# Softmax cross-entropy, first load cut at partition 16, labels behind the table load, last sums in PSUM with refitted pieces

## The chip, the cores and the metric

One core of one Trainium2 chip. The metric is the device time of one execution in microseconds. Runs of the kernel before on one chip agree within about 0.6 us in 2431 (0.03%). By the record's 95% intervals (about 0.15% to either side of a ratio) effects of a few tenths count as no difference; they are read here from five rounds and from traces, and are only as sure as that.

In the profile's lines ACT is ScalarE, DVE is VectorE, POOL is GpSimd and SP the engine that issues the logit loads. HBM is the memory that the logits come from; SBUF and PSUM are the core's two on-chip memories. A packet is what one DMA engine moves in one piece, here a row's part of a load. A load lands when its last byte is reported in.

## The reference

```python
batch, seq, vocab = 16, 512, 32000          # fp32 logits, labels
logits_max = np.max(logits, axis=-1, keepdims=True)
log_sum_exp = np.log(np.sum(np.exp(logits - logits_max), axis=-1)) + logits_max.squeeze(-1)
log_probs = logits - log_sum_exp[..., np.newaxis]
loss = -log_probs[np.arange(batch)[:, None], np.arange(seq), labels]
```

1.05 GB of logits are read once; the result is 8192 numbers. The kernel leaves out the maximum (the logits are normal draws).

## The kernel before

The 8192 rows are split over 128 partitions, 64 rows each ("groups" g = 0..63). Row p*64+g goes to partition p, so a load takes 128 rows that lie 8.19 MB apart. Groups are loaded in two halves of 16000 columns into three buffers in turn; ScalarE does exp in place and sums each half with its accumulator. The loads of the first group and of the last two are shorter.

```python
P = 128; G = 64; W = 16000
lg_pg = lg.rearrange("(p g) v -> p g v", g=G)

plan(0, [[4000, 4000, 8000], [16000]], [(0, 0), (0, 1), (0, 2), (1, 0)])
for g in range(1, G - 2):
    plan(g, [[W], [W]], [(0, 0), (1, 0)])
for g, i, at, n in [                          # group, buffer, column in it, width
    (G - 2, 0, 0, 12000), (G - 2, 1, 0, 11000), (G - 2, 2, 0, 9000),
    (G - 1, 3, 0, 8720), (G - 1, 2, 9000, 6470), (G - 1, 3, 8720, 4700),
    (G - 1, 4, 0, 3410), (G - 1, 3, 13420, 2550), (G - 1, 4, 3410, 1910), (G - 1, 4, 5320, 1455),
    (G - 1, 4, 6775, 1135), (G - 1, 4, 7910, 905), (G - 1, 4, 8815, 745),
]: ...
sums = persist.tile([P, G - 1, 5], FP32)      # SBUF
sums_last = persist.tile([P, K], FP32)        # SBUF, K = 10
nc.scalar.dma_start(out=labs64[:], in_=labels_pg)
nc.scalar.preload_act_table_set("natural_log_exp_and_others")
nc.vector.memset(sums[:], 0.0)
# ... gathers, index lists (cut)
for j, (g, b, at, n) in enumerate(loads):
    load = nc.sync.dma_start(out=t[:, at:at + n], in_=lg_pg[:, g, c0:c0 + n])
    # ... semaphores, pick of the label's logit (cut)
    nc.scalar.activation(out=ap, in_=ap, func=EXP, accum_out=s)
    if left == 1:
        nc.vector.reduce_sum(out=part[:], in_=sums_last[:, 0:K - 1], axis=X)
nc.scalar.activation(out=logsum_last[:], in_=sums_last[:, K - 1:K], func=LN, bias=part[:])
# ... subtract, store (cut)
```

The softmax here doesn't subtract the row's maximum and nothing guards it: scores larger than these inputs give would overflow.

Of the kernel before, what the change touches and what calls it, by code (L numbers as in the profile page):

```python
# [9 lines left out]
FP32 = mybir.dt.float32  # L10
# [4 lines left out]
LN = mybir.ActivationFunctionType.Ln  # L15
ALU = mybir.AluOpType
X = mybir.AxisListType.X
# [3 lines left out]
def kernel(  # L21
# [6 lines left out]
    nc = tc.nc  # L28

    B, S, V = logits.shape  # L30
    P = 128
    G = B * S // P
    W = 16000
# [3 lines left out]
    lg_pg = lg.rearrange("(p g) v -> p g v", g=G)  # L37
# [7 lines left out]
    def plan(g, widths_by_buffer, order):  # L45

        n_buffers = 1 + max((l[1] for l in loads), default=-1)
        for b, i in order:
            ws = widths_by_buffer[b]
            loads.append((g, n_buffers + b, sum(ws[:i]), ws[i]))  # L50

    plan(0, [[4000, 4000, 8000], [16000]], [(0, 0), (0, 1), (0, 2), (1, 0)])
    for g in range(1, G - 2):
        plan(g, [[W], [W]], [(0, 0), (1, 0)])
    b = loads[-1][1] + 1
    for g, i, at, n in [
        (G - 2, 0, 0, 12000), (G - 2, 1, 0, 11000), (G - 2, 2, 0, 9000),
        (G - 1, 3, 0, 8720), (G - 1, 2, 9000, 6470), (G - 1, 3, 8720, 4700),
        (G - 1, 4, 0, 3410), (G - 1, 3, 13420, 2550), (G - 1, 4, 3410, 1910), (G - 1, 4, 5320, 1455),
        (G - 1, 4, 6775, 1135), (G - 1, 4, 7910, 905), (G - 1, 4, 8815, 745),  # L60
    ]:
        loads.append((g, b + i, at, n))
    assert sum(l[3] for l in loads) == G * V
# [2 lines left out]
    persist = ctx.enter_context(tc.tile_pool(name="persist", bufs=1))  # L66
# [24 lines left out]
    own = persist.tile([P, NB * 2, NI], FP32)  # L91
# [1 line left out]
    in_first = persist.tile([P, G], mybir.dt.int32)  # L93
    picks = ctx.enter_context(tc.tile_pool(name="picks", bufs=2))
    K = 10
    sums = persist.tile([P, G - 1, 5], FP32)
    sums_last = persist.tile([P, K], FP32)
    totals = persist.tile([P, G - 1], FP32)
    logsum = persist.tile([P, G - 1], FP32)
    res = persist.tile([P, G - 1], FP32)  # L100
    part = persist.tile([P, 1], FP32)
    logsum_last = persist.tile([P, 1], FP32)
    res_last = persist.tile([P, 1], FP32)

    ctx.enter_context(tc.manual_schedule())


    nc.scalar.dma_start(out=labs64[:], in_=labels_pg)
    nc.scalar.preload_act_table_set("natural_log_exp_and_others")  # L109
    nc.vector.memset(sums[:], 0.0)  # L110
    nc.gpsimd.iota(idx[:], pattern=[[V, G]], base=0, channel_multiplier=G * V)
    nc.gpsimd.tensor_tensor(out=idx[:], in0=idx[:], in1=labs32, op=ALU.add)  # L112
    nc.gpsimd.iota(part16[:], pattern=[[0, 1]], base=0, channel_multiplier=1)
    nc.gpsimd.iota(entries[:], pattern=[[1, NI]], base=0, channel_multiplier=0, allow_small_or_imprecise_dtypes=True)
    for g in gathered:
        nc.gpsimd.indirect_dma_start(  # L116
            out=lab_logit[:, g:g + 1],
            out_offset=None,
            in_=lg,
# [6 lines left out]
    for q in range(3):  # L126
        nc.vector.tensor_scalar(  # L127
            out=mine[:, q:q + 1], in0=part16f[:], scalar1=4.0 * q, scalar2=None, op0=ALU.add
        )
    for n in (12.0, 6.0):  # L130
        nc.vector.tensor_scalar(  # L131
            out=mine_at[:], in0=mine[:], scalar1=n, scalar2=n, op0=ALU.is_ge, op1=ALU.mult
# [3 lines left out]
    for q in range(3):  # L136
        nc.vector.tensor_scalar(  # L137
            out=mine_at[:, q:q + 1], in0=mine[:, q:q + 1], scalar1=16.0 * q, scalar2=None, op0=ALU.mult
# [4 lines left out]
        out=one_hot[:], in0=entries[:], scalar1=at_entry[:], scalar2=None, op0=ALU.is_equal  # L143
    )
    nc.vector.tensor_scalar(
        out=clamped[:, 0, :], in0=labs32, scalar1=float(W - 1), scalar2=None, op0=ALU.min
    )
    nc.vector.tensor_scalar(
        out=clamped[:, 1, :], in0=labs32, scalar1=float(-W), scalar2=0.0, op0=ALU.add, op1=ALU.max
    )  # L150
    nc.vector.tensor_scalar(
        out=in_first[:], in0=labs32, scalar1=float(W), scalar2=None, op0=ALU.is_lt
    )
    for h in range(2):
        for q in range(3):
            nc.vector.tensor_scalar(  # L156
                out=lists[:, :, h, q], in0=clamped[:, h, :], scalar1=mine[:, q:q + 1], scalar2=None, op0=ALU.mult
# [6 lines left out]
    buffers = {}  # L164
    col = {}
    n_exp = {}
    full_in = [tc.alloc_semaphore(f"full{i}_in") for i in range(3)]
    n_full = [0, 0, 0]
    spaces = [data.tile([P, W], FP32, tag=f"t{i}", name=f"t{i}") for i in range(3)]
    exps = []  # L170

    def exp(g, ap):
        k = n_exp.get(g, 0)
        n_exp[g] = k + 1
        s = sums[:, g, k:k + 1] if g < G - 1 else sums_last[:, k:k + 1]
        return nc.scalar.activation(out=ap, in_=ap, func=EXP, accum_out=s)  # L176

    for j, (g, b, at, n) in enumerate(loads):
        if b not in buffers:
            buffers[b] = spaces[b % 3]  # L180
        t = buffers[b]
        c0 = col.get(g, 0)
        col[g] = c0 + n
        load = nc.sync.dma_start(out=t[:, at:at + n], in_=lg_pg[:, g, c0:c0 + n])  # L184
        if n == W:
            n_full[b % 3] += 1
            loaded = (full_in[b % 3], 16 * n_full[b % 3])
        else:
            loaded = (tc.alloc_semaphore(f"short{j}_in"), 16)
        load.then_inc(loaded[0], 16)  # L190
        tc.no_tile_sem_insts.add(load.ins.name)
        users = []
        if g in picked:
            h = c0 // W
            i = picked.index(g) % NB
            if h == 0 and i == 0:
                pk = picks.tile([P, NB * 2, NI], FP32, tag="pk", name="pk")
            pick = nc.gpsimd.indirect_copy(  # L198
                out=pk[:, 2 * i + h, :], data=t[:], idxs=lists[:, g, h, 0:3], i_know_this_is_slow=True
            )  # L200
            users.append(pick)
        users.append(exp(g, t[:, at:at + n]))
        users[0]._wait_ge(*loaded)
        tc.add_to_no_dep_group(f"load{j}", load.ins)
        tc.declare_no_dep(users[0].ins, load.ins, reason="waits for the load's own semaphore")
        tc.declare_fence(users[0].ins, group=f"load{j}")
        exps.append(users[-1])
        if g in picked and h == 1 and i == NB - 1:
            nc.vector.copy_predicated(own[:], one_hot[:].unsqueeze(1).to_broadcast([P, NB * 2, NI]), pk[:])  # L209
            nc.vector.reduce_sum(  # L210
                out=found[:, :, g - NB + 1:g + 1].rearrange("p h g -> p g h"),
                in_=own[:].rearrange("p (g h) n -> p g h n", h=2),
                axis=X,
            )

        left = len(loads) - 1 - j
        if left == 9:
            nc.vector.reduce_sum(out=totals[:], in_=sums[:], axis=X)  # L218
            lo, hi = picked[0], picked[-1] + 1
            nc.vector.tensor_copy(out=lab_logit[:, lo:hi], in_=found[:, 1, lo:hi])  # L220
            nc.vector.copy_predicated(lab_logit[:, lo:hi], in_first[:, lo:hi], found[:, 0, lo:hi])  # L221
        if left == 8:
            nc.scalar.activation(out=logsum[:], in_=totals[:], func=LN)  # L223
            nc.vector.tensor_tensor(out=res[:], in0=logsum[:], in1=lab_logit[:, 0:G - 1], op=ALU.subtract)  # L224
        if left == 1:
            nc.vector.reduce_sum(out=part[:], in_=sums_last[:, 0:K - 1], axis=X)  # L226
    assert n_exp[G - 1] == K
    nc.sync.dma_start(out=out_pg[:, 0:G - 1], in_=res[:])

    nc.scalar.activation(out=logsum_last[:], in_=sums_last[:, K - 1:K], func=LN, bias=part[:])  # L230
    nc.vector.tensor_tensor(out=res_last[:], in0=logsum_last[:], in1=lab_logit[:, G - 1:G], op=ALU.subtract)  # L231
    nc.sync.dma_start(out=out_pg[:, G - 1:G], in_=res_last[:])

# [29 lines left out]
```

## Time and profile before

| | before |
|---|---|
| time, median (runs) | 2430.91 us (6) |
| span of the profiled run | 2428.7 us |
| share of the span that the logit queue holds the DMA engines | 99.9% |
| last landing of logits | 2424.71 us |

The GB/s row of the page cuts the span in 40 slices of 60.7 us; a slice shows what the engines moved. It is flat from the first slice on, so the start and the end are the only places where anything can be won or lost.

```profile
GB/s 423 438 422 438 438 424 437 438 433 427 438 437 423 439 436 426 436 438 432 428 438 435 425 438 436 428 434 436 434 428 436 437 426 436 437 429 433 436 430 383
```

The same start in wider windows (DMA share and GB/s stand last; a packet is booked where it starts):

```profile
5.00:10.00 5.00, 0.99 (x8) 1.90 (x1) 1.27 (x4) 1.00 1.03 440
10.00:20.00 10.00, 3.52 (x19) 5.36 (x4) 3.40 (x4) 1.00 1.04 440
30.00:40.00 10.00, 0.00 (x0) 0.00 (x0) 0.00 (x0) 1.00 0.95 410
```

### The profile page before, as it was taken

The numbers are of one execution on the slowest core, as the hardware profiler recorded it, in microseconds if no ns is written. First come the engines' busy times: TensorE is split into PE (matmuls) and PEld (weight loads), VectorE is DVE, ScalarE is ACT, GpSimd is POOL, SyncE is SP. The second block draws the span as 40 slices with busy tenths as digits, with TensorE's granted clock in tenths as the row PEclk, the third lists the DMA queues.
The fourth block names the chain that finished last, engine by engine and source line by source line (L and its number), as shares of the span: only waits on it lengthen the run. The fifth ranks groups of instructions, "written<-read, shape, count | busy, mean of one in ns | idle before, by whom it ended". The sixth has DMA issues, their size and how long they took to land.

```text
span 2428.7 us, 667 instructions
## 1 busy us (share of the span) xinstructions
DVE 20.5 (1%) x45; ACT 1748.7 (72%) x281; POOL 86.7 (4%) x132
## 2 busy tenths in 40 slices
DVE  0000000000000000000000000000000000000000
ACT  4777767777677767777677776777767776777778
POOL 0000000000000000000000000000000000000000
DMA  9999999999999999999999999999999999999999
GB/s 423 438 422 438 438 424 437 438 433 427 438 437 423 439 436 426 436 438 432 428 438 435 425 438 436 428 434 436 434 428 436 437 426 436 437 429 433 436 430 383
DMA packets 20580, 1048.72 MB, mean 432 GB/s; under 512 B 2656, under 2 KB 2784, under 8 KB 3424
## 3 DMA queue, kind: packets, MB, share of 16 engines
q1 hardware_dynamic: 20304, 1048.62, 99.9%
q10 hardware_dynamic: 144, 0.07, 0.0%
q0 software_dynamic: 128, 0.00, 0.0%
q14 instruction: 4, 0.03, 0.0%
HBM read 1048.64 MB, written 0.03 MB: 432 GB/s over the span
## 4 chain that ended last, share of the span: by engine, by line
DMA 71%; ACT 23%; issue 4%; POOL 1%; SPq 0%; POOLq 0%; DVE 0%
DMA t<-in_logits_dram 71%; ACT t L176 23%; POOL pk L198 1%; SPq L184 0%; POOLq L258 0%; ACT logsum_last L230 0%; DVE res_last L231 0%; POOLq L198 0%
## 5 line engine op out<-in xcount | busy, mean ns | idle before, releaser
L176 ACT ACTIVATE t<-t 128x16000 f32<-128x16000 f32 (+6 forms) x139 | 1734.8, 12480 | 676.2 <-POOL pk L198 635.1
L198 POOL INDIRECT_COPY pk<-t,lists 128x48 f32 x120 | 81.6, 680 | 2216.1 <-DMA t<-in_logits_dram 2216.1
L209 DVE COPY_PREDICATED own<-one_hot,pk 128x960 f32<-128x960 int32 x6 | 7.4, 1233 | 2286.0 <-POOL pk L198 2286.0
L176 ACT ACTIVATION_READ_ACCUMULATOR t<-t 128x1 f32 x139 | 25.9, 186 | 0.0
L210 DVE TENSOR_REDUCE found<-own 128x20 f32<-128x960 f32 x6 | 6.9, 1155 | 0.2
L116 POOL DMA_INDIRECT lab_logit<-in_logits_dram,idx x4 | 4.1, 1034 | 1.2 <-issue 0.9
L109 ACT ACT_TABLE_LOAD x1 | 1.3, 1283 | 1.2 <-PEq L247 1.2
L156 DVE TENSOR_SCALAR lists<-clamped,mine 128x64 uint16<-128x64 f32 x6 | 1.2, 368 | 0.0
L218 DVE TENSOR_REDUCE totals<-sums 128x63 f32<-128x315 f32 x1 | 0.5, 481 | 79.6 <-ACT t L176 79.6
L159 DVE MEMSET own<- 128x960 f32 x1 | 0.9, 858 | 0.1
L112 POOL TENSOR_TENSOR idx<-idx,labs 128x64 int32<-128x64 int32 x1 | 0.3, 321 | 7.4 <-DMA labs<-in_labels_dram 7.4
L224 DVE TENSOR_TENSOR res<-logsum,lab_logit 128x63 f32<-128x63 f32 x1 | 0.2, 225 | 15.2 <-ACT logsum L223 15.2
L142 DVE TENSOR_SCALAR one_hot<-entries,at_entry 128x48 int32<-128x48 f32 x1 | 0.3, 347 | 0.1
L131 DVE TENSOR_SCALAR mine_at<-mine 128x3 f32<-128x3 f32 x2 | 0.3, 169 | 0.1
L110 DVE MEMSET sums<- 128x315 f32 x1 | 0.3, 321 | 0.9 <-PEq L247 0.9
L134 DVE TENSOR_TENSOR mine<-mine,mine_at 128x3 f32<-128x3 f32 x2 | 0.3, 162 | 0.1
L230 ACT ACTIVATE logsum_last<-sums_last,part 128x1 f32<-128x1 f32 x1 | 0.3, 294 | 0.0
L226 DVE TENSOR_REDUCE part<-sums_last 128x1 f32<-128x9 f32 x1 | 0.2, 162 | 14.5 <-ACT t L176 14.5
L137 DVE TENSOR_SCALAR mine_at<-mine 128x1 f32<-128x1 f32 x3 | 0.3, 146 | 0.0
L127 DVE TENSOR_SCALAR mine<-part16f 128x1 f32<-128x1 f32 x3 | 0.3, 147 | 0.0
L223 ACT ACTIVATE logsum<-totals 128x63 f32<-128x63 f32 x1 | 0.2, 238 | 0.0
L221 DVE COPY_PREDICATED lab_logit<-in_first,found 128x60 f32<-128x60 int32 x1 | 0.2, 232 | 0.0
(17 smaller groups left out, 2.7 us busy)
## 6 DMA issues: line engine op xcount, KB each, us to landing
t<-in_logits_dram SPq DMA_DIRECT2D x123, 8000.0 KB, 41.6
t<-in_logits_dram SPq DMA_DIRECT2D x1, 6000.0 KB, 36.8
t<-in_logits_dram SPq DMA_DIRECT2D x1, 5500.0 KB, 32.4
t<-in_logits_dram SPq DMA_DIRECT2D x1, 4500.0 KB, 24.2
t<-in_logits_dram SPq DMA_DIRECT2D x1, 4360.0 KB, 23.7
t<-in_logits_dram SPq DMA_DIRECT2D x2, 2000.0 KB, 9.5
t<-in_logits_dram SPq DMA_DIRECT2D x1, 4000.0 KB, 21.1
t<-in_logits_dram SPq DMA_DIRECT2D x1, 3235.0 KB, 31.0
```

The costliest lines, as they stand in the source:

```text
L109: nc.scalar.preload_act_table_set("natural_log_exp_and_others")
L110: nc.vector.memset(sums[:], 0.0)
L112: nc.gpsimd.tensor_tensor(out=idx[:], in0=idx[:], in1=labs32, op=ALU.add)
L116: nc.gpsimd.indirect_dma_start(out=lab_logit[:, g:g + 1], out_offset=None, in_=lg, in_offset=bass.IndirectOffsetOnAxis(ap=idx[:, g:g + 1], ...
L127: nc.vector.tensor_scalar(out=mine[:, q:q + 1], in0=part16f[:], scalar1=4.0 * q, scalar2=None, op0=ALU.add)
L156: nc.vector.tensor_scalar(out=lists[:, :, h, q], in0=clamped[:, h, :], scalar1=mine[:, q:q + 1], scalar2=None, op0=ALU.mult)
L159: nc.vector.memset(own[:], 0.0)
L176: return nc.scalar.activation(out=ap, in_=ap, func=EXP, accum_out=s)
L198: pick = nc.gpsimd.indirect_copy(out=pk[:, 2 * i + h, :], data=t[:], idxs=lists[:, g, h, 0:3], i_know_this_is_slow=True)
L209: nc.vector.copy_predicated(own[:], one_hot[:].unsqueeze(1).to_broadcast([P, NB * 2, NI]), pk[:])
L210: nc.vector.reduce_sum(out=found[:, :, g - NB + 1:g + 1].rearrange("p h g -> p g h"), in_=own[:].rearrange("p (g h) n -> p g h n", h=2), a ...
L218: nc.vector.reduce_sum(out=totals[:], in_=sums[:], axis=X)
```

## The change

Its intent: let the first transfer carry 16 rows, one for each of the 16 DMA engines, so that all start at once, and the other 112 rows follow while those run; keep the small label packets out of the first load's way; let ScalarE write the last sums into PSUM, hoped to be cheaper, spread over banks (as the second index of the tile, 0 to 7, is called here); and refit the last pieces to that. The sums of the last group's first three pieces go to bank 0, each later one to the next bank, the tenth to bank 7. Lines left out are marked with dots.

```diff
-    plan(0, [[4000, 4000, 8000], [16000]], [(0, 0), (0, 1), (0, 2), (1, 0)])
-    for g in range(1, G - 2):
+    for g in range(G - 2):
         plan(g, [[W], [W]], [(0, 0), (1, 0)])
...
-        (G - 1, 4, 6775, 1135), (G - 1, 4, 7910, 905), (G - 1, 4, 8815, 745),
+        (G - 2, 0, 0, 11250), (G - 2, 1, 0, 10750), (G - 2, 2, 0, 10000),
+        (G - 1, 3, 0, 9150), (G - 1, 3, 9150, 6630), (G - 1, 2, 10000, 4775),
+        (G - 1, 4, 0, 3420), (G - 1, 4, 3420, 2495), (G - 1, 4, 5915, 1715), (G - 1, 4, 7630, 1380),
+        (G - 1, 4, 9010, 1035), (G - 1, 4, 10045, 790), (G - 1, 4, 10835, 610),
...
-    sums_last = persist.tile([P, K], FP32)
+    sums_last = psum.tile([P, 8, 512], FP32, tag="sums_last", name="sums_last")
+    place_last = [(max(0, k - 2), min(k, 2) if k <= 2 else 0) for k in range(K)]
...
+    nc.scalar.preload_act_table_set("natural_log_exp_and_others")
     nc.scalar.dma_start(out=labs64[:], in_=labels_pg)
-    nc.scalar.preload_act_table_set("natural_log_exp_and_others")
     nc.vector.memset(sums[:], 0.0)
+    nc.vector.memset(sums_last[:, :, 0:K - 7], 0.0)
...
-        load = nc.sync.dma_start(out=t[:, at:at + n], in_=lg_pg[:, g, c0:c0 + n])
+        cuts = [0, 16, P] if j == 0 else [0, P]
+        parts = [
+            nc.sync.dma_start(out=t[p0:p1, at:at + n], in_=lg_pg[p0:p1, g, c0:c0 + n])
+            for p0, p1 in zip(cuts, cuts[1:])
+        ]
...
-            nc.vector.reduce_sum(out=part[:], in_=sums_last[:, 0:K - 1], axis=X)
+            nc.vector.reduce_sum(out=partial[:], in_=sums_last[:, 0:7, 0:K - 7], axis=mybir.AxisListType.XY)
...
-    nc.scalar.activation(out=logsum_last[:], in_=sums_last[:, K - 1:K], func=LN, bias=part[:])
+    nc.scalar.activation(out=logsum_last[:], in_=sums_last[:, 7, 0:1], func=LN, bias=partial[:])
```

More of the change, by code (lines that the diff above doesn't have):

```diff
@@ L56 @@
     for g, i, at, n in [
-        (G - 2, 0, 0, 12000), (G - 2, 1, 0, 11000), (G - 2, 2, 0, 9000),
-        (G - 1, 3, 0, 8720), (G - 1, 2, 9000, 6470), (G - 1, 3, 8720, 4700),
-        (G - 1, 4, 0, 3410), (G - 1, 3, 13420, 2550), (G - 1, 4, 3410, 1910), (G - 1, 4, 5320, 1455),
-        (G - 1, 4, 6775, 1135), (G - 1, 4, 7910, 905), (G - 1, 4, 8815, 745),
+        (G - 2, 0, 0, 11250), (G - 2, 1, 0, 10750), (G - 2, 2, 0, 10000),
+        (G - 1, 3, 0, 9150), (G - 1, 3, 9150, 6630), (G - 1, 2, 10000, 4775),
+        (G - 1, 4, 0, 3420), (G - 1, 4, 3420, 2495), (G - 1, 4, 5915, 1715), (G - 1, 4, 7630, 1380),
+        (G - 1, 4, 9010, 1035), (G - 1, 4, 10045, 790), (G - 1, 4, 10835, 610),
     ]:
@@ L95 @@
     K = 10
-    sums = persist.tile([P, G - 1, 5], FP32)
-    sums_last = persist.tile([P, K], FP32)
+    psum = ctx.enter_context(tc.tile_pool(name="psum", bufs=1, space=bass.MemoryType.PSUM))
+    sums = persist.tile([P, G - 1, 3], FP32)
+    sums_last = psum.tile([P, 8, 512], FP32, tag="sums_last", name="sums_last")
+    place_last = [(max(0, k - 2), min(k, 2) if k <= 2 else 0) for k in range(K)]
     totals = persist.tile([P, G - 1], FP32)
@@ L100 @@
     res = persist.tile([P, G - 1], FP32)
-    part = persist.tile([P, 1], FP32)
+    partial = persist.tile([P, 1], FP32)
     logsum_last = persist.tile([P, 1], FP32)
@@ L166 @@
     n_exp = {}
-    full_in = [tc.alloc_semaphore(f"full{i}_in") for i in range(3)]
-    n_full = [0, 0, 0]
+    first_in = [tc.alloc_semaphore(f"first{i}_in") for i in range(3)]
+    count_in = [0, 0, 0]
     spaces = [data.tile([P, W], FP32, tag=f"t{i}", name=f"t{i}") for i in range(3)]
-    exps = []
     def exp(g, ap):
@@ L174, in exp @@
         n_exp[g] = k + 1
-        s = sums[:, g, k:k + 1] if g < G - 1 else sums_last[:, k:k + 1]
+        if g < G - 1:
+            s = sums[:, g, k:k + 1]
+        else:
+            bank, at = place_last[k]
+            s = sums_last[:, bank, at:at + 1]
         return nc.scalar.activation(out=ap, in_=ap, func=EXP, accum_out=s)
@@ L183 @@
         col[g] = c0 + n
-        load = nc.sync.dma_start(out=t[:, at:at + n], in_=lg_pg[:, g, c0:c0 + n])
-        if n == W:
-            n_full[b % 3] += 1
-            loaded = (full_in[b % 3], 16 * n_full[b % 3])
-        else:
-            loaded = (tc.alloc_semaphore(f"short{j}_in"), 16)
-        load.then_inc(loaded[0], 16)
-        tc.no_tile_sem_insts.add(load.ins.name)
+        cuts = [0, 16, P] if j == 0 else [0, P]
[3 more added lines that the diff above has]
+        ]
+        if at == 0:
+            count_in[b % 3] += 16 * len(parts)
+            loaded = (first_in[b % 3], count_in[b % 3])
+        else:
+            loaded = (tc.alloc_semaphore(f"load{j}_in"), 16)
+        for part in parts:
+            part.then_inc(loaded[0], 16)
+            tc.no_tile_sem_insts.add(part.ins.name)
         users = []
@@ L203 @@
         users[0]._wait_ge(*loaded)
-        tc.add_to_no_dep_group(f"load{j}", load.ins)
-        tc.declare_no_dep(users[0].ins, load.ins, reason="waits for the load's own semaphore")
+        for part in parts:
+            tc.add_to_no_dep_group(f"load{j}", part.ins)
+            tc.declare_no_dep(users[0].ins, part.ins, reason="waits for the load's own semaphore")
         tc.declare_fence(users[0].ins, group=f"load{j}")
-        exps.append(users[-1])
         if g in picked and h == 1 and i == NB - 1:
```

## The prediction

Passages that no trace or run of this case supports are cut from the text below, where marked. The first rival (one in five; "the clash" further down) was that the transfer on 16 neighbouring partitions would itself be slow and hold what is queued behind it. The sum stands as written, 0.30 + 0.16 = 0.46 us. Of the 0.16, 0.11 is the shorter last piece (step 5), less the 0.03 of step 4; two terms for single accesses of PSUM made up the rest, and these are cut, so the terms that can still be read come to 0.30 + 0.11 - 0.03 = 0.38. The 0.042 us a read in step 4 was not shown by any run when it was written.

> **What bounds the kernel now.** I read the page first: engine shares, then the DMA row, the chain and the DMA issues.
>
> ```profile
> span 2428.7 us, 667 instructions
> DVE 20.5 (1%) x45; ACT 1748.7 (72%) x281; POOL 86.7 (4%) x132
> ...
> q1 hardware_dynamic: 20304, 1048.62, 99.9%
> ...
> HBM read 1048.64 MB, written 0.03 MB: 432 GB/s over the span
> ...
> t<-in_logits_dram SPq DMA_DIRECT2D x123, 8000.0 KB, 41.6
> ```
>
> No compute engine is near full, and the queue of the logit loads holds the 16 DMA engines for 99.9% of the span. A load of 8000 KB lands 41.6 us after its issue, more than two loads' worth (the trace has them landing 18.9 us apart: 60.38, 79.27, 117.08 less 98.19), so the queue never runs dry. In the trace's packet records a row of 64,000 B takes 2.366 us on its engine (27.05 GB/s); an engine has 8 rows of 64 groups with 2 halves, 1024 such rows, 1024 x 2.366 = 2423 us. The body can't be shortened without moving fewer bytes, and the change moves the same bytes. What is left is the start, where the engines wait for their first packet, and the end, after the last byte. So I looked at both closely.
>
> Start, in windows (columns: DMA share and GB/s stand last):
>
> ```profile
> 1.50:1.75 0.25, 0.00 (x0) 0.25 (x1) 0.00 (x0) 1.00 0.00 0
> 1.75:2.00 0.25, 0.00 (x0) 0.25 (x1) 0.00 (x0) 1.00 4.80 960
> 2.00:2.50 0.50, 0.00 (x0) 0.45 (x1) 0.00 (x0) 1.00 0.13 32
> 2.50:3.00 0.50, 0.00 (x0) 0.00 (x0) 0.00 (x0) 1.00 0.17 66
> 3.00:3.50 0.50, 0.00 (x0) 0.00 (x0) 0.00 (x0) 1.00 1.10 462
> ```
>
> Packets are booked where they start. The first load is issued at 0.74 us; all 16 engines start their first packet between 1.76 and 2.03, and there is no hole to fill before the next ones near 3: by the packet records the first 16,000 B packets take 0.87 to 1.54 us where later ones take 0.596, and the second ones follow at once, behind the label packets (27 to 39 ns each, 8 an engine). The first load pieces have all landed at 22.77 us (8.19 MB); at the later pace that is 18.9, so about 1.4 us is lost after the first packet's start, of it 0.3 us labels (8 x 0.033), the rest slow first packets and stagger.
>
> The end, in the timeline:
>
> ```profile
> 2422.73 1.15 ACT L176 ACTIVATE t<-t 128x1135 f32<-128x1135 f32 x1
> 2423.78 0.19 ACT L176 ACTIVATION_READ_ACCUMULATOR t<-t 128x1 f32 x1
> 2423.87 0.94 ACT L176 ACTIVATE t<-t 128x905 f32<-128x905 f32 x1
> 2424.72 0.19 ACT L176 ACTIVATION_READ_ACCUMULATOR t<-t 128x1 f32 x1
> 2424.81 0.81 ACT L176 ACTIVATE t<-t 128x745 f32<-128x745 f32 x1
> ...
> 2425.53 0.19 ACT L176 ACTIVATION_READ_ACCUMULATOR t<-t 128x1 f32 x1
> 2425.75 0.29 ACT L230 ACTIVATE logsum_last<-sums_last,part 128x1 f32<-128x1 f32 x1
> 2426.07 0.16 DVE L231 TENSOR_TENSOR res_last<-logsum_last,lab_logit 128x1 f32<-128x1 f32 x1 [0.97 <-ACT logsum_last L230]
> 2426.26 0.34 SPq L232 DMA_DIRECT2D out_dram<-res_last  x1
> ```
>
> No ACT line after 2404.31 has a wait in brackets, so ACT looks like the bound of the tail. The landings in the trace say it is a tie: the last eight pieces land at 2409.94, 2414.01, 2417.11, 2419.47, 2421.28, 2422.70, 2423.79 and 2424.71; their exps start 0.11, 0.14, 0.07, 0.02, 0.02, 0.03, 0.08 and 0.10 us later. A faster ACT alone would gain the 0.10 at most, then wait for DMA. After the start of the last exp come 3.9 us in series: exp, accumulator read, log, subtraction, store.
>
> [...] 745 columns give 0.186 + 0.621 = 0.807 (shown 0.81), and exp starts lie 0.833n + 0.186 apart (3410 to 2550: 3.03), which is 0.093 for each of the exp and its accumulator read. [...]
>
> **The change, part by part.**
> 1. First group as two whole loads. It removes two of the three short pieces. Per engine, 16 packets of 596 and 8 of 1185 ns (19.02 us) become 8 of 2366 (18.93): 0.09 us. The first exp starts near 22 instead of 8.1 us and ends near 36; its buffer is wanted again only for the fourth load, and two loads (until about 60 us) are queued by then. No stall.
> 2. First load cut at partition 16. The first issue has 16 rows to describe, not 128; issues at the start last 0.38 to 0.42 us, and first packets start 0.6 after the issue's end. I estimate 0.1 to 0.2 us earlier, and the stagger of 0.27 us mostly gone. [...]
> 3. Labels after the table load. The same 8 packets per engine, so the same 0.3 us, only later. Each now has a 2.37 us row between it and the next in place of 0.6, so labels land near 20 us instead of 8.25. Their users (four gathers, index lists) are wanted at 61 us and at the end. Worth 0 to 0.1 us, by leaving the first issue alone. Together the start gives, by my choice, 0.3 us of DMA finishing earlier (0.09 + 0.15 + 0.06 of stagger and contention).
> 4. Sums in PSUM. If each read saves 0.042 us, the exp interval becomes 0.833n + 0.144: nine intervals save 0.38 us of ACT time. The refit spends that: the group's first piece grows 430 columns, its landing moves back by 430 x 1.182 ns (8 x 2.366 us/16000) = 0.51 us. Working backwards from the last landing with 8 packets a piece, and forwards on ACT with 0.144, the last exp is ready 0.13 us after its landing, where it was 0.10. So the last exp begins 0.03 later than now, relative to the DMA.
> 5. The last piece shrinks from 745 to 610 columns: 135 x 0.833 = 0.11 us. [...] The vector reduction of seven banks runs under the last exp, as now (0.16 us beside 0.81).
> 6. The two memsets and the narrower sums are off the path.
> Sum: 0.30 + 0.16 = 0.46, rounded to 0.5 us.
>
> **Rivals.**
> - [...] a refit done to tenths of a microsecond would hardly stand beside such a loss. One in five.
> - PSUM saves nothing per piece. ACT then finishes 0.38 later, and the gain shrinks to about 0.1: 2430.7.
> - The start gains nothing [...]: 2430.6.
> - The start gains the whole loss but the labels, some 1 us: 2429.6.
>
> **Range and chances.** Nothing touches the 18.9 us pace[...]. The ordinary outcomes lie between 2429.4 and 2431.0; I set the range from 2429.2 to 2432.0 and leave the clash outside it, which is why it is not better than eight in ten. Chances: faster 0.004, same 0.992, slower 0.004.
>
> **What would show it.** First packets starting before 1.7 us and taking about 3 us each (right)[...]. Landing of the first whole load near 22.4, of the second near 41.2 (41.49 now). ACTIVATION_READ_ACCUMULATOR of the last group at about 0.144 us in place of 0.186, exp starts 0.833n + 0.144 apart. Last landing near 2424.4, last log near 2425.2. It would be wrong if a mid-run load lands more than 18.9 us after its neighbour, if the tail's exps show waits on DMA, or if the reduction waits for the last exp.

## The result

The changed kernel takes 2451.02 us (median of 6 runs, 2450.53 to 2451.55) against 2430.91 us, 20 us more and far outside the predicted range. The ratio is 1.0083 (95% interval 1.0070 to 1.0096), so by the 2% rule it counts as the same.

The DMA row (busy share of the engines, 9 is 90% or more) and the GB/s row of the changed kernel's page, slices of 61.2 us:

```profile
span 2449.7 us, 664 instructions
...
DMA  9999999999999999999999999999999999999998
GB/s 281 432 432 432 432 433 435 435 435 435 435 435 433 434 434 430 433 432 434 434 435 435 435 435 435 434 432 434 431 431 434 434 434 435 435 434 435 435 429 378
```

Only the first slice differs: 281 in place of 423. At some 433 GB/s a slice of 61.2 us should have moved (433 - 281) x 61.2 = 9.3 MB more, which is 21.5 us of transfer. The whole loss is there. Note what the busy digits do not show: the DMA busy share of that slice is still 90% or more. A packet counts as busy from its start to its end, so an engine with a slow packet looks as busy as one with a fast one. Windows of the changed kernel's start show where:

```profile
0.00:5.00 5.00, 0.29 (x2) 1.28 (x1) 0.39 (x5) 1.00 1.67 205
5.00:10.00 5.00, 0.00 (x0) 0.00 (x0) 0.00 (x0) 1.00 0.26 42
10.00:20.00 10.00, 4.51 (x26) 0.00 (x0) 4.67 (x7) 1.00 0.93 191
20.00:30.00 10.00, 0.00 (x0) 0.00 (x0) 0.00 (x0) 1.00 1.16 307
30.00:40.00 10.00, 0.00 (x0) 0.00 (x0) 0.00 (x0) 1.00 0.90 205
40.00:50.00 10.00, 0.00 (x0) 5.31 (x1) 0.00 (x0) 1.00 1.02 397
```

The share stays near 1 while the rate is half (0.90 with 205 GB/s from 30 to 40 us, where the kernel before has 0.95 with 410). The 42 GB/s is nearly an empty window: in its 5 us hardly any packet starts, because the first sixteen last that long. The trace's packet records give each packet's duration; all are of 64,000 B, and they are taken here sixteen at a time in order of start (the records name neither engine nor partition):

| n-th packets | start us | median us | least to most |
|---|---|---|---|
| 1 (the 16 rows) | 1.75 to 3.07 | 8.47 | 7.40 to 9.33 |
| 2 | 9.8 to 12.0 | 5.08 | 4.83 to 5.85 |
| 3 | 15.4 to 16.8 | 4.65 | 4.63 to 4.78 |
| 4 | 20.0 to 21.5 | 3.22 | 2.95 to 4.57 |
| 5 | 23.4 to 25.8 | 3.70 | 3.63 to 4.43 |
| 6 | 27.1 to 29.5 | 4.49 | 4.14 to 4.61 |
| 7 | 31.3 to 34.1 | 4.66 | 4.60 to 4.79 |
| 8 | 36.0 to 38.7 | 4.19 | 4.15 to 4.74 |
| any later whole load, from its second packets on | | 2.37 | |

So the first transfer and also the second, of 112 rows, are slow in all their packets. The exps answer to it. Kernel before (the third line is that of its fourth piece, the second half of group 0):

```profile
8.10 3.54 ACT L176 ACTIVATE t<-t 128x4000 f32<-128x4000 f32 x1 [5.66 <-DMA t<-in_logits_dram]
...
22.79 6.87 ACT L176 ACTIVATE t<-t 128x8000 f32<-128x8000 f32 x1 [6.33 <-DMA t<-in_logits_dram]
...
41.51 13.54 ACT L176 ACTIVATE t<-t 128x16000 f32<-128x16000 f32 x1 [11.76 <-DMA t<-in_logits_dram]
```

Changed kernel:

```profile
44.69 13.54 ACT L182 ACTIVATE t<-t 128x16000 f32<-128x16000 f32 x1 [42.67 <-DMA t<-in_logits_dram]
...
63.46 13.54 ACT L182 ACTIVATE t<-t 128x16000 f32<-128x16000 f32 x1 [5.13 <-DMA t<-in_logits_dram]
```

The second half of group 0 can be worked on at 63.46 in place of 41.51, 21.95 us later; the last logits land at 2445.75 in place of 2424.71, 21.0 us later. The loss is made in the first 44 us and nothing gives it back.

### The profile page after: what moved, and what is told of

Same layout as the page of the kernel before. It is cut to its first block, busy times and chain, and to the rows that moved or that the text cites. A ratio compares the mean times of both kernels' runs of the same rounds, so it can differ in the third digit from the quotient of the medians.

```text
span 2449.7 us, 664 instructions
## 1 busy us (share of the span) xinstructions
DVE 20.4 (1%) x46; ACT 1747.8 (71%) x277; POOL 87.1 (4%) x132
## 4 chain that ended last, share of the span: by engine, by line
DMA 71%; ACT 24%; issue 3%; POOL 1%; another core or an unknown queue 0%; SPq 0%; DVE 0%; ACTq 0%; POOLq 0%
DMA t<-in_logits_dram 71%; ACT t L182 24%; POOL pk L210 1%; SPq L193 0%; ACT logsum_last L242 0%; DVE res_last L243 0%; ACT logsum L235 0%; ACTq L182 0%; POOLq L210 0%
## 5 line engine op out<-in xcount | busy, mean ns | idle before, releaser
L182 ACT ACTIVATE t<-t 128x16000 f32<-128x16000 f32 (+4 forms) x137 | 1734.2, 12662 | 698.5 <-POOL pk L210 633.9
L236 DVE TENSOR_TENSOR res<-logsum,lab_logit 128x63 f32<-128x63 f32 x1 | 0.2, 226 | 15.4 <-ACT logsum L235 15.4
## 6 DMA issues: line engine op xcount, KB each, us to landing
t<-in_logits_dram SPq DMA_DIRECT2D x1, 5375.0 KB, 31.3
```

The costliest lines, as they stand in the source:

```text
L182: return nc.scalar.activation(out=ap, in_=ap, func=EXP, accum_out=s)
```

## The experiments

My theory after the result: the rival that the prediction had, on both parts of the cut. I supposed that the pace of a transfer depends on which partitions of SBUF it writes, that both the 16 and the 112 rows are slow for that, and that since all engines carry such a transfer, what is queued behind it waits. Why partitions should matter I had not from these runs; they do not show it. Forecasts made from it: the 4.7 to 5 us a packet in E3, E5 and E13 are about twice the 2.37 us of a later packet. Rivals: something else of the change; a fixed price of the cut; uneven rows per engine; rows far apart in HBM.

**E1: the changed kernel without the cut.**

```diff
-        cuts = [0, 16, P] if j == 0 else [0, P]
+        cuts = [0, P]
```

> The changed kernel with its first load issued whole (128 partitions) and nothing else undone. [...] the whole loss goes; first whole load lands near 22.5 us in place of 44.67, span about 21.9 us shorter than the changed kernel's 2449.7, time 2430 to 2430.8. Rival (the loss comes from the whole-width first group, the later labels or the new tail): the time stays above 2440 us.

Measured: 2430.46 us (5 runs) against 2431.09 for the kernel before on the same chip. The first load lands at 22.47. So the cut alone costs about 2451.02 - 2430.46 = 20.6 us, and the rest of the change gains about half a microsecond. Its start in windows, beside the changed kernel's above:

```profile
5.00:10.00 5.00, 0.00 (x0) 0.00 (x0) 0.00 (x0) 1.00 1.10 477
10.00:20.00 10.00, 0.00 (x0) 0.00 (x0) 0.00 (x0) 1.00 1.01 439
```

**E2: the kernel before with its first load (4000 columns) cut** (semaphores left out here).

```diff
-        load = nc.sync.dma_start(out=t[:, at:at + n], ...)
+        cuts = [0, 16, P] if j == 0 else [0, P]
+        parts = [nc.sync.dma_start(out=t[p0:p1, at:at + n], ...) for p0, p1 in zip(cuts, cuts[1:])]
```

> The kernel before with only its first load, 4000 columns wide, cut at partition 16. [...] the loss is a rate, so it scales with the bytes: a quarter of the 22 us that 16000 columns lost, so +5 to +6 us, about 2436.4; first packets near 2.3 us in place of 1.3. Rival (a fixed price of the cut[...]): +20 us, as with the wide load.

Measured: 2434.24 us against 2431.09, +3.15. Not a fixed price of 20 us, but less than the quarter of it that I had expected, and the first packets took 1.29 us in the median (0.76 to 1.79), as uncut (1.30); the second ones 1.08 to 1.95, where uncut ones take 0.60. The effect grows with the bytes but not in proportion: a part of it does not show with short packets. Why was not pursued.

**E3: cut at 64.**

```diff
-        cuts = [0, 16, P] if j == 0 else [0, P]
+        cuts = [0, 64, P] if j == 0 else [0, P]
```

> The changed kernel with the first load cut at partition 64 in place of 16. [...] all 8 packets of an engine take about 4.7 us, the first load lands near 2 + 38 = 40 us (+18 over the whole load), time about 2449. Rival (only the tiny first transfer of 16 rows hurts, or only an uneven 7 rows an engine): two halves of 4 rows an engine cost nothing, time near 2431.

Measured: 2450.93 us. The packets of the first load take 4.5 to 5.4 us throughout, and the rate stands at half for 40 us:

```profile
10.00:20.00 10.00, 0.00 (x0) 0.00 (x0) 0.00 (x0) 1.00 1.00 205
20.00:30.00 10.00, 0.00 (x0) 0.00 (x0) 0.00 (x0) 1.00 1.00 205
30.00:40.00 10.00, 0.00 (x0) 0.00 (x0) 0.00 (x0) 1.00 1.00 205
40.00:50.00 10.00, 0.00 (x0) 6.15 (x1) 0.00 (x0) 1.00 0.97 397
```

Two even halves of 64 rows, four packets for each of 16 engines, neither tiny nor odd, lose as much as 16 + 112. The rivals of size and of uneven rows fall.

**E4: the first 16 partitions read neighbouring rows of HBM** (16 losses computed from other rows; with this many random logits the result still passes the comparison).

```diff
-            nc.sync.dma_start(out=t[p0:p1, at:at + n], in_=lg_pg[p0:p1, g, c0:c0 + n])
+            nc.sync.dma_start(
+                out=t[p0:p1, at:at + n],
+                in_=lg[0:16, 0:n] if p1 == 16 else lg_pg[p0:p1, g, c0:c0 + n],
+            )
```

> The changed kernel, but its first 16 partitions read 16 neighbouring rows of HBM (128,000 B apart) in place of rows 8.19 MB apart; wrong result for 16 losses on purpose. [...] the first 16 packets still take 7.4 to 9.3 us. Rival (rows far apart in HBM [...]): they take about 3 us, and the first load lands 6 us sooner.

Measured: first packets 7.5 to 9.0 us, time 2450.66 us (one run). Where these 16 rows lie in memory is not it; that leaves where they go.

**E5: eight transfers of 16 partitions, spaced by 8** (the edit in short).

```diff
+            nc.sync.dma_start(out=t[k:P:8, at:at + n], in_=lg_pg[k:P:8, g, c0:c0 + n])
+            for k in range(8)
```

> The first load as eight transfers of 16 partitions each, every eighth partition (0, 8, .. 120; then 1, 9, .. 121; and so on). [...] a 64,000 B packet takes about 4.7 to 5 us, the whole load lands near 2 + 8 x 5 = 42 us, and the time is about 2451. Rival (any transfer of 16 rows is slow, whatever its partitions): 8 to 9 us a packet, the load lands near 75 us, time about 2483. Second rival (neighbouring partitions alone are slow): about 2.4 us a packet and 2431.

Measured: 2451.05 us; packets 4.1 to 5.6 us for the first transfer (4.65 in the median), then 5.0. The same 16 rows' worth of bytes takes 8.5 us in the median on partitions 0..15 and 4.65 on partitions 0, 8, .. 120: the choice of partitions sets the pace.

**E6 and E7: the tail alone, and the start alone without the cut.** E6 is E1 with the first group's pieces and the label order of the kernel before; E7 is the kernel before with E1's start.

```diff
# E7, against the kernel before
-    plan(0, [[4000, 4000, 8000], [16000]], [(0, 0), (0, 1), (0, 2), (1, 0)])
-    for g in range(1, G - 2):
+    for g in range(G - 2):
...
-    nc.scalar.dma_start(out=labs64[:], in_=labels_pg)
     nc.scalar.preload_act_table_set("natural_log_exp_and_others")
+    nc.scalar.dma_start(out=labs64[:], in_=labels_pg)
```

> The kernel before with only the new tail (sums in PSUM, refitted pieces); its start, label order and narrow first pieces kept. E1 (whole first load, new tail) was 0.63 us faster than the kernel before: 0.2 us inside the span and 0.33 us outside it (time less span 1.85 in place of 2.2). If the tail gives all of the inside part, the span here is about 2428.5 (0.2 less). If the time outside the span comes from the start (labels after the table load), time less span stays 2.2 and the gain is 0.2 us; if it comes from the tail, the gain is 0.5 to 0.6 us.

> The kernel before with only the new start less the cut (first group as two whole loads, labels after the table load); its old tail kept. If the start's gain inside the span is nil (third load landed at 60.59 us in E1 and 60.38 before), the span stays near 2428.7; my prediction's 0.3 us would make it 2428.4. Time less span 1.85 if the label order or the fewer loads cause it (gain about 0.35 us), 2.2 if not (gain about 0).

Measured on one chip: before 2430.92, E6 2430.61 (-0.31), E7 2430.86 (-0.06, inside the scatter). Time less span, that is, the part of the device time that the profile doesn't show, is 1.8 us in all runs of E6 and 2.2 in all of E7. So the start gives nothing, and in E6 the gain lies outside the span: its span is no shorter in the median (2428.8 against 2428.7).

**E8: the PSUM banks in reverse order.**

```diff
-    place_last = [(max(0, k - 2), min(k, 2) if k <= 2 else 0) for k in range(K)]
+    place_last = [(7 - max(0, k - 2), min(k, 2) if k <= 2 else 0) for k in range(K)]
```

(with the sum over banks 1 to 7 and the log reading bank 0)

> E1 with the order of the PSUM banks reversed: the last piece's sum goes to bank 0, the first three to bank 7. In E1 the accumulator read of the last group grows from 0.15 us (bank 0) to 0.21 us (bank 7) and the short exps by 0.04. If the bank's number does it, the reads now shrink from 0.21 to 0.15 and the last exp to the log takes about 0.74 us in place of 0.84: 0.06 to 0.10 us faster than E1. If the shorter pieces do it, nothing changes.

Measured: 2430.46 us, as E1; the reads grow from 0.15 to 0.21 us as before, though now into banks 7 down to 0. The bank does not matter. What does is not settled, since the pieces get shorter in the order in which they come: E12's ninth read lasts 0.206 us behind 835 columns and E1's ninth 0.204 behind 790, so the place in the row fits better than the length.

**E9: E1 with an extra load of 16 rows in front.**

```diff
+    extra = nc.sync.dma_start(out=spaces[2][0:16, :], in_=lg_pg[0:16, G - 1, 0:W])
```

(The buffer is overwritten later by the third load, which waits for a VectorE read of it; that read and the semaphores are left out here.)

> E1 (first load whole) with one more load of 16 partitions by 16000 columns put in front of it, into a buffer that is overwritten later; 1.02 MB more than the work needs. If all 16 engines are held [...], it costs a whole slow packet each, 9.0 to 9.5 us more than E1, about 2439.8, and the whole load behind it runs at full pace (packets of 2.4 us) at once. If only the bytes count, or if the engines work ahead on other rows, it costs 2.4 us, 2432.9. In the first case 7 of the 22 us are the 16 rows' (9.4 less the 2.4 that those rows need anyway) and 15 are the 112 rows'.

Measured: 2439.57 us, 9.1 more than E1, which ran on another chip (8.8 if each is taken against the kernel before on its own chip). First packets 7.5 to 9.1 us, then one packet of 2.6 to 3.8 an engine, as at E1's start (2.7 to 3.5), and 2.4 from there on. The second row, beside the changed kernel's 191 GB/s, shows the whole load behind the 16 rows at full rate:

```profile
5.00:10.00 5.00, 0.00 (x0) 0.00 (x0) 0.00 (x0) 1.00 0.08 15
10.00:20.00 10.00, 4.51 (x27) 0.00 (x0) 4.65 (x7) 1.00 1.07 409
```

Some 6.7 us is waiting (9.1 less the 2.4 us that a later packet takes).

**E10 and E11: what saves time outside the span, and what PSUM saves.** E10 adds an unused, zeroed PSUM tile to the kernel before; E11 is E1 with the last sums in SBUF.

```diff
# E10, against the kernel before
+    unused = psum.tile([P, 8, 512], FP32, tag="unused", name="unused")
+    nc.vector.memset(unused[:, :, 0:K - 7], 0.0)
# E11, against E1
-    sums_last = psum.tile([P, 8, 512], FP32, tag="sums_last", name="sums_last")
+    sums_last = persist.tile([P, 8, 3], FP32)
```

> The kernel before with a PSUM tile that is allocated and zeroed and never used. E6 and E1 showed time less span at 1.8 where the kernels without PSUM have 2.2. If having a PSUM tile in the program does that, time less span is 1.85 here and the time falls by about 0.35 us; if not, both stay (2.2, 2430.9).

> E1 with the last group's sums kept in SBUF, pieces as refitted. My step: a sum read into PSUM saves about 0.042 us an exp, nine on the way to the last one. So exp starts lie 0.833n + 0.186 apart again, the last exp starts 0.35 to 0.4 us later than E1's 2424.84, and the span grows by 0.3 to 0.4 us. Rival (the saving is only in the record): no change.

Measured on one chip (before: 2431.38): E10 2430.76, E11 2430.71. Time less span is 1.8 to 1.9 in both, so PSUM is not the cause: E11 has none. What they share with E1 and E6 is a second VectorE memset at the start (E16 below). On PSUM itself, the tails, first E1:

```profile
2414.95 3.04 ACT L182 ACTIVATE t<-t 128x3420 f32<-128x3420 f32 x1
2417.89 0.16 ACT L182 ACTIVATION_READ_ACCUMULATOR t<-t 128x1 f32 x1
2417.94 2.28 ACT L182 ACTIVATE t<-t 128x2495 f32<-128x2495 f32 x1
...
2424.84 0.75 ACT L182 ACTIVATE t<-t 128x610 f32<-128x610 f32 x1
2425.02 0.18 DVE L238 TENSOR_REDUCE partial<-sums_last 128x1 f32<-128x21 f32 x1 [13.90 <-ACT t L182]
2425.44 0.21 ACT L182 ACTIVATION_READ_ACCUMULATOR t<-t 128x1 f32 x1
2425.68 0.26 ACT L242 ACTIVATE logsum_last<-sums_last,partial 128x1 f32<-128x1 f32 x1
```

then E11:

```profile
2414.97 3.04 ACT L181 ACTIVATE t<-t 128x3420 f32<-128x3420 f32 x1
2417.91 0.19 ACT L181 ACTIVATION_READ_ACCUMULATOR t<-t 128x1 f32 x1
2418.01 2.27 ACT L181 ACTIVATE t<-t 128x2495 f32<-128x2495 f32 x1
...
2425.11 0.70 ACT L181 ACTIVATE t<-t 128x610 f32<-128x610 f32 x1
2425.71 0.19 ACT L181 ACTIVATION_READ_ACCUMULATOR t<-t 128x1 f32 x1
2425.93 0.29 ACT L241 ACTIVATE logsum_last<-sums_last,partial 128x1 f32<-128x1 f32 x1
```

From the exp of 3420 columns to the next takes 2.99 us with PSUM and 3.04 with SBUF: 0.14 and 0.19 above the 2.85 that the columns take. The saving per exp is real, 0.04 to 0.05 us, and the last exp starts 0.27 us earlier. From that start to the log, though, PSUM takes 0.84 us and SBUF 0.82: behind the last exp the read is not shorter. In time, E11 is 0.25 us behind E1 (another chip), and 0.29 behind E12 below, which ran on E11's chip with the sums in PSUM and other pieces; 0.3 to 0.4 was expected.

**E12: pieces fitted again.**

```diff
-        (G - 1, 3, 0, 9150), (G - 1, 3, 9150, 6630), (G - 1, 2, 10000, 4775), ...
+        (G - 1, 3, 0, 9070), (G - 1, 3, 9070, 6480), (G - 1, 2, 10000, 4730),
+        (G - 1, 4, 0, 3420), (G - 1, 4, 3420, 2500), (G - 1, 4, 5920, 1840), (G - 1, 4, 7760, 1390),
+        (G - 1, 4, 9150, 1060), (G - 1, 4, 10210, 835), (G - 1, 4, 11045, 675),
```

> E1 with the pieces fitted to what E1 shows: the exps of its last eight pieces start 0.2 to 0.35 us after their landing, so its tail is bound by ScalarE from the first piece on. Pieces 9070, 6480, 4730, 3420, 2500, 1840, 1390, 1060, 835, 675 should bring each exp to 0.05 to 0.15 us after its landing. The last exp then starts 0.15 to 0.2 us earlier and is 0.05 longer: 0.10 to 0.15 us faster than E1, about 2430.3.

Measured: 2430.42 us on a chip where the kernel before took 2431.38. The last exp still starts 0.25 us after its landing (0.30 in E1), so the fit missed its aim, and its span of 2428.6 in the median is E1's. It beats the kernel before, as E1 does; it is not shown to beat E1, which ran on another chip.

**E13 and E14: do slow packets pace a whole transfer?** As E9, with 9 partitions (0, 4, .. 32) or 8 (0, 4, .. 28). The question was whether E13's ninth row makes two packets slow or all nine, E14 being the control.

```diff
# E13
+    extra = nc.sync.dma_start(out=spaces[2][0:36:4, :], in_=lg_pg[0:36:4, G - 1, 0:W])
# E14
+    extra = nc.sync.dma_start(out=spaces[2][0:32:4, :], in_=lg_pg[0:32:4, G - 1, 0:W])
```

> E1 with one more load in front, of 9 partitions 0, 4, .. 32 by 16000 columns (scratch, overwritten later). [...] two first packets take about 4.7 to 5 us and seven about 3 us (as E1's first). [...] all nine take about 5 us; that would explain why all engines ran at half pace through the 112 rows.

> The control: the same with 8 partitions 0, 4, .. 28[...]. All eight first packets about 3 us, time 2.4 us above E1's 2430.5. If small transfers are slow [...] they take 5 us or more, as the 16 neighbouring partitions did (8.5).

Measured: E14's eight packets take 2.74 to 3.22 us, time 2433.41. E13 has two packets of 4.68 and 4.80 us and seven of 3.27 to 3.74, time 2434.40 (one run each). One more partition makes two packets slow and not nine; which two is not shown, since the records name no partition. E14 shows that small transfers are not slow as such. E13 also speaks against what I offered for the 112 rows, that a few slow packets pace all engines of a transfer: seven of its packets took 3.27 to 3.74 us beside the two of 4.68 and 4.80. A different ninth partition was not tried, so nine rows as such are not excluded.

**E15 and E17: the 112 rows alone, from far and from near rows.**

```diff
# E15
+    extra = nc.sync.dma_start(out=spaces[2][16:P, :], in_=lg_pg[16:P, G - 1, 0:W])
# E17
+    extra = nc.sync.dma_start(out=spaces[2][16:P, :], in_=lg[0:112, 0:W])
```

> E1 with one more load in front, of partitions 16 to 127 by 16000 columns (scratch): the second part of the cut alone, without the 16 rows ahead of it. [...] 7 packets an engine take 31 to 33 us, time about 2462; [...] if the 112 rows are slow only behind the 16, 16.6 us, about 2447.

> E15 with the extra 112 rows read from neighbouring rows of HBM (128,000 B apart) in place of rows 8.19 MB apart; the destination is unchanged. If the destination partitions set the pace, packets stay at 3 to 4.7 us and the time at 2461.5; if it is where the rows lie in HBM, packets take 2.4 us and the time is about 2447.

Measured: E15 2461.47 us, 31.0 more than E1, where the bytes need 16.6; its seven packets an engine take 3.0 to 4.7 us in the median, as in the changed kernel. E17 2460.53, the same but for 1 us (one run each). So the 112 rows are slow by themselves, and where they lie in HBM is not the reason. The waits add up: 6.7 us (E9) and 31.0 - 16.6 = 14.4 us (E15) make 21.1, against the 20.6 us that E1 shows for the cut.

**E16: the kernel before with one more memset.**

```diff
+    unused = persist.tile([P, 24], FP32)
     nc.vector.memset(sums[:], 0.0)
+    nc.vector.memset(unused[:], 0.0)
```

> The kernel before with one more VectorE memset of a small unused SBUF tile. Time less span is 2.2 in the kernels with one memset at the start and 1.8 in those with two (E10 unused PSUM tile, E11 sums in SBUF). If one more VectorE instruction is what does it, time less span is 1.85 and the time 0.35 us less; if not, 2.2 and no change.

Measured: 2430.47 us against 2430.91; time less span 1.79 to 1.87 in all five runs, 2.15 to 2.24 in all nine of the kernel before. An instruction that does nothing useful saves 0.35 us outside the span. Why stays open; the trace has no record of that time.

## Why the prediction was wrong

- **What bounds the kernel** (transfers, end to end) was right; that is why 20 us at the start went through to the end undiminished.
- **Step 2, "First load cut at partition 16", failed.** It said "I estimate 0.1 to 0.2 us earlier" and let the 112 rows run free behind the first packets. The first issue takes 0.39 us with 16 rows and 0.38 with 128 in the kernel before, and the first packets start at 1.75 us with and without the cut, so nothing was won, and their stagger grew (1.75 to 3.07 us, where it was 1.76 to 2.03 before); and the cut cost 20.6 us (E1), some 6.7 as waiting in the 16 rows' transfer and 14.4 in that of the 112. The 16 rows held all engines for 7.4 to 9.3 us, where the prediction had about 3 us a packet.
- **The rival had the right place, but was mis-sized and mis-weighed.** It priced the 16 rows alone, and these cost 6.7 us (E9). The 112 rows are slow too: 31 us measured where 16.6 would do, 14.4 more (E15). That term I did not work out at all. The objection that a carefully refitted change "would hardly stand beside such a loss" was a guess about how the change came about, not a reading of the profile. Where the rows lie in HBM does not matter (first packets of 7.5 to 9.0 us in E4, 7.4 to 9.3 in the changed kernel; 2460.53 us in E17, 2461.47 in E15), the partitions they go to do (packets of 4.5 to 5.4 us in E3, 4.65 in E5 where 0..15 take 8.5, two slow ones of nine in E13, none of eight in E14).
- **Still open**: why the packets to some sets of partitions are slow, and why the 112 rows take 31 us; in E13 the two slow packets did not bring the other seven to their pace.
- **Steps 1 and 3**: 0.3 us of earlier transfers was predicted, E7 shows none within its scatter (-0.06 us); the second whole load landed at 41.67 us there, where 41.2 was predicted and 41.49 was measured before. The "about 1.4 us" said to be lost at the start doesn't follow from the figures beside it: 22.77 - 1.76 - 18.9 is 2.1. The labels landed at 13.1 us in the changed kernel and 22.6 in E1 ("near 20"), without harm, as predicted.
- **Steps 4 and 5**: exp starts 0.144 above the columns' time were right (0.14, E1 against E11). The last exp started 0.30 us after its landing, not 0.13; of that, 0.10 is already in the second piece, which starts 0.10 after its landing; where the rest comes from was not traced. The reads took 0.15 to 0.21 us, not 0.144. The 0.19 us to be saved in series after that start (0.11 of it the shorter piece, the rest the cut terms) became 0.13 (from the last exp's start to the log's end 1.23 before, 1.10 in E1): the shorter piece's 0.11 and 0.03 on the log (0.26 against 0.29) came, on the read nothing did (0.21 against 0.19), and the last exp's own record grew (0.75 in PSUM, 0.70 in SBUF, E11).
- **The sum without the cut**, 0.46 us, is close to E1's 0.63, but that is luck: some 0.35 is the extra memset's, outside the span (E16), which the prediction put "off the path" and gave nothing.

## What to carry to other kernels

In a kernel like this one keep a transfer to SBUF on all 128 partitions; to make it start small, cut it in columns, as the kernel before does (2430.92 us, 2430.86 uncut in E7), and not in partitions: here parts of 16, 64 and 112 partitions had packets of 7.4 to 9.3, 4.5 to 5.4 and 3.0 to 5.9 us where a later whole load has 2.37, held all engines, and what was queued behind waited (9.1 us for 16 rows in E9). When you have a rival explanation, size all of its terms, and do not discount it because somebody seems to have taken care. And look at the rate beside the busy share: engines with slow packets look busy (a share of 1.00 with 205 GB/s, E3).
